# HGRN2 mixer of a decoder trunk: two heads in step, scores in 32-token blocks on four column groups, values and gates 512 columns wide

## The chip, the cores and the metric

The kernel runs on one core of one Trainium2 chip. Its time is the device time of one execution in microseconds (us); the median of three runs is given. A profile is of one execution. The engines are TensorE (PE in the profile; its weight loads are PEld), VectorE (DVE), ScalarE (ACT), GpSimd (POOL) and SyncE (SP), which here issues the DMAs. Each engine takes its instructions in the order in which they are written for it and waits on semaphores for the others.

## What is computed

Two layers over 512 tokens of 1024 features: a Mamba-2 mixer with an MLP and a gated embedding, then an HGRN2 mixer with the same two behind it. The change lies in the HGRN2 mixer, which has eight heads of 128 keys and 128 values:

```python
def hgrn2_mixer(u, w_in, lb, norm_w, w_out):
    q, fz, v, g = jnp.split(u @ w_in, 4, axis=-1)
    log_f = jnp.logaddexp(jnp.log(lb), jnp.log1p(-lb) + jax.nn.log_sigmoid(fz))
    k = (1.0 - lb) * jax.nn.sigmoid(-fz)
    ...
    def step(s_prev, inp):
        q_, kk, v_, b_ = inp
        diff = b_[:, :, None] - b_[:, None, :]
        dec = jnp.exp(jnp.where(mask, diff, -jnp.inf))
        scores = jnp.einsum('blhk,bshk,blshk->bhls', q_, kk, dec)
        o = jnp.einsum('bhls,bshv->blhv', scores, v_) + jnp.einsum('blhk,bhkv->blhv', q_ * jnp.exp(b_), s_prev)
        b_last = b_[:, -1]
        s_new = jnp.exp(b_last)[..., None] * s_prev + jnp.einsum(
            'bshk,bshv->bhkv', kk * jnp.exp(b_last[:, None] - b_), v_)
        return s_new, o
    ...
    o = rms_norm(o, norm_w).reshape(bsz, seq, D_MODEL) * jax.nn.silu(g.astype(jnp.float32))
    return o.astype(u.dtype) @ w_out
```

The score of a query token and an earlier key token is a sum over 128 keys of query times key times the product of all gates between the two. All arithmetic is fp32.

## The kernel before

Large products are made of three fp32r products each (`mm3`, lines 118 to 120): high part times high part, high times low, low times high. `unit` (L101) loads a weight tile of 128x1024 (512 KB) and splits it, ACT writing the high part `whi` (L112) and DVE the low part `wlo` (L114). There are three buffers for raw tiles and six each for `whi` and `wlo`. Tiles in the profile are named by their tags: `pj`, `py`, `pt`, `pm` are PSUM banks (four, two, one, one), `b` is a buffer of a split activation.

The mixer keeps 128 keys on the partitions and the 512 tokens along the free axis, in four chunks of 128. `qf` (L783) projects a head's queries and gates into tiles `xs` (q), `sz` (the gate f) and `cv` (k). `vg` (L762) projects values and gates for a pair of heads, with the activations as stationary operand and 256 weight columns moving (L775), and evacuates them by 512 columns (L777).

`hcore` (L846) works one head. It builds the scores of a chunk by levels: at level m, blocks of 2 to the m tokens are paired, and only the scores of a second block's queries with a first block's keys are new. In between the keys and queries of all blocks are multiplied by the gates' products (L912 for keys, L913 for queries, L916 for the products), so that a plain matrix product gives the decayed score.

- The diagonal and levels 0 and 1 are elementwise products, summed over the keys by a product with a matrix of ones, after a split (`column_sums`, L859; split at L861 and L862, product at L866).
- Levels 2 to 4 take full 128x128 products of a chunk in fp32 (`scores`, L852, product at L856), of which masks pick what is new (L927).
- Levels 5 and 6 (blocks of 32 and 64) multiply only the blocks needed (L901); ACT copies them (L931).
- Then keys are turned (L936, copied to `btok` at L938), states made (L943, L945, L947), outputs made (L954, L956), normalised and gated (L961 to L966), turned back (L972) and split (L973, L974).

What sets the order on TensorE is written out by hand: inside `manual_schedule` each `yield` of `hcore` tells how many us of background work to put there (`FILL`), and `fill` (L838) takes that much from `background` (L817): the projections of later heads, in the order of `JOBS`, and last `out0` (L803), the output projection of the first four heads. Two heads are worked at a time, an even one and an odd one at different stages. The order on the other engines is the scheduler's, with weight tiles pulled ahead. Behind the mixer come the output projection of the last four heads (L1003), the layer norm and the second MLP.

Of the kernel before, what the change touches and what calls it, by code (L numbers as in the profile page):

```python
# [9 lines left out]
F32R = mybir.dt.float32r  # L10
# [15 lines left out]
NLEV = 7  # L26
# [17 lines left out]
def trunk(ctx: ExitStack, tc, a):  # L44
# [30 lines left out]
    bufs = dict(ssd=dict(two, ss=2), mlp0=mlp, hgrn=dict(two, xs=4, sz=4, cv=4, y=2, pv=2, btok=2), mlp1=mlp)  # L75
# [667 lines left out]
    lmask = mk(cpool, [P, 6, P], "lmask", U8)  # L743
    lmf = mk(w4, [P, 6, P], "a")
    nc.sync.dma_start(lmf, a["lmask"])
    nc.vector.tensor_copy(lmask, lmf)
    ones_r = mk(cpool, [P, P], "ones_r", F32R)
    nc.scalar.activation(ones_r, ident, AF.Identity, scale=0.0, bias=one)
# [13 lines left out]
    def vg(i):  # L762

        res = []
        for which in range(2):
            units = [unit(a["whvg"][4 * i + 2 * which + j]) for j in range(2)]
            t = mk(w4, [P, NCH, 256], "ab"[which])
            for c2 in range(2):
                ps = bank(psj, "pj")
                for c in range(2):  # L770
                    sl = slice((2 * c2 + c) * P, (2 * c2 + c + 1) * P)
                    for k in range(8):
                        hi, lo = units[k // 4]
                        ks = slice((k % 4) * 256, (k % 4 + 1) * 256)
                        mm3(ps[:, c * 256 : (c + 1) * 256], x_s.h(k, sl), x_s.l(k, sl), hi[:, ks], lo[:, ks], k == 0, k == 7)  # L775
                        yield 0.33
                nc.scalar.activation(  # L777
                    t[:, 2 * c2 : 2 * c2 + 2, :].rearrange("p c f -> p (c f)"), ps, AF.Silu if which else AF.Copy
                )
            res.append(t)  # L780
        made["vg", i] = res

    def qf(h):  # L783
        ps = []
        for w in range(2):
            hi, lo = unit(a["whq"][2 * h + w])
            ps.append(bank(psj, "pj"))
            for k in range(8):
                c = slice(k * P, (k + 1) * P)
                mm3(ps[w], hi[:, c], lo[:, c], x_s.h(k), x_s.l(k), k == 0, k == 7)  # L790
                yield 0.65
            if w == 0:
                q = tmp("xs", [P, T])
                nc.scalar.copy(q, ps[0])
        f = tmp("sz", [P, T])
        nc.scalar.activation(f, ps[1], AF.Sigmoid)
        nc.scalar.activation(f, f, AF.Identity, scale=lbc[:, h : h + 1], bias=lb[:, h : h + 1])
        kk = tmp("cv", [P, T])
        nc.scalar.activation(kk, ps[1], AF.Sigmoid, scale=-1.0)
        nc.scalar.activation(kk, kk, AF.Copy, scale=lbc[:, h : h + 1])  # L800
        made["qf", h] = q, f, kk

    def out0():  # L803
        for h in range(2):
            units = [unit(a["who"][2 * h + i]) for i in range(2)]
            for c in range(NCH):
                sl = slice(c * P, (c + 1) * P)
                ps = bank(psj, "pj")
                for k in range(4):
# [3 lines left out]
                    yield 0.65  # L813
# [3 lines left out]
    def background():  # L817
        first = vg(0)
        for _ in range(FIRST_V):
            yield next(first)  # L820
        for f in late:
            f()
        yield from qf(0)
        yield from qf(1)
        yield from first
        for job in JOBS:
            yield from {"v": vg, "q": qf}[job[0]](int(job[1])) if job != "o" else out0()
# [18 lines left out]
    def hcore(h, s, i, hl):  # L846
        vs = slice((h % 2) * P, (h % 2 + 1) * P)
        q, f, kk = need("qf", h)
        sc = tmp("cm", [P, NCH, P])
        py = lambda: bank(psy, "py%d" % (h % 2))  # L850

        def scores():  # L852
            pc = py()
            for c in range(NCH):
                sl = slice(c * P, (c + 1) * P)
                nc.tensor.matmul(pc[:, sl], kk[:, sl], q[:, sl], start=True, stop=True)  # L856
            return pc.rearrange("p (c l) -> p c l", c=NCH)

        def column_sums(f, n):  # L859

            nc.scalar.copy(hl[:, 0, :n], f)  # L861
            nc.vector.tensor_sub(hl[:, 1, :n], f, f32(hl[:, 0, :n]))  # L862
            pc = py()
            yield FILL[0]
            for r in range(2):
                nc.tensor.matmul(pc[:, :n], ones_r, hl[:, r, :n], start=r == 0, stop=r == 1)  # L866
            return pc[:, :n].rearrange("p (c l) -> p c l", c=NCH)


        qk = tmp("cbm", [P, T])  # L870
        nc.vector.tensor_mul(qk, q, kk)
        nc.vector.tensor_mul(q, q, f)
        pc = yield from column_sums(qk, T)
        nc.vector.tensor_mul(sc, pc, bc(ident, 1, NCH))
        qk = tmp("cbm", [P, T])
        two = lambda t: t.rearrange("p (b two) -> p b two", two=2)
        nc.vector.tensor_mul(qk[:, : T // 2], two(q)[:, :, 1], two(kk)[:, :, 0])
        tot = f
        tots = tmp("y", [P, T])
        toff = 0  # L880
        for m in range(NLEV):
            half = 1 << m
            if m == 0:
                pc = yield from column_sums(qk[:, : T // 2], T // 2)
            elif m == 1:
                qk = tmp("cbm", [P, T])
                quads = lambda t: t.rearrange("p (b two u) -> p b two u", two=2, u=2)
                nc.vector.tensor_mul(
                    qk.rearrange("p (b l s) -> p b l s", l=2, s=2),
# [234 lines left out]
```

## Time and profile before

| | us |
|---|---|
| median of three runs | 1473.4 (1472.41 to 1473.43) |
| span of the profiled execution | 1471.1 |
| TensorE busy | 1455.5 |
| VectorE busy | 1076.6 |
| ScalarE busy | 731.8 |

The mean granted TensorE clock of the profiled execution is 0.998. The matmuls are pipelined: one of 128x512 is shown with about 0.39 us, while the next starts 0.227 us after it, so the work of TensorE is read from the starts. An fp32 matmul is shown as two records with a weight load each, an fp32r one as a single record.

### The profile page before, as it was taken

Reading aid. Unit: us, or ns where it says so; the run is one execution under the profiler, and the core shown is the slowest. Engines: PE = TensorE matmul, PEld = TensorE weight load, DVE = VectorE, ACT = ScalarE, POOL = GpSimd, SP = SyncE. Lnnn points to the kernel's source line nnn. Section 1 sums busy time; section 2 is a strip of 40 time slices with the busy share of each in tenths; the row PEclk is TensorE's granted clock in tenths of the full one; section 3 lists DMA queues with packets and bytes.
Section 4 is the critical chain, followed back from the end, with each engine's and each line's share of the span. In section 5 each row is a group of like instructions: output and inputs, shape, how many; then the busy total and the mean of one; then the engine's idle time right before and its main releaser. Section 6 shows DMA issues by size and latency. Waiting matters only on the chain.

```text
span 1471.1 us, 19578 instructions
## 1 busy us (share of the span) xinstructions
PE 1455.5 (99%) x7720; PEld 1223.5 (83%) x7720; DVE 1076.6 (73%) x1685; ACT 731.8 (50%) x1053; POOL 0.9 (0%) x9
## 2 busy tenths in 40 slices
PE   8999999999999999999999999999999999999998
PEld 6788888887888888888888998988888888888887
DVE  6999687787967667677845767768786766667873
ACT  5887455563264444545534453543346454444551
POOL 0000000000000000000000000000000000000000
PEclk9999999999999999999999999999999999999999
DMA  6343323233434434442413212222423434434231
GB/s 252 122 139 115 118 98 115 101 109 121 144 115 143 144 129 151 135 166 80 152 58 117 98 60 72 72 72 73 172 86 112 141 135 147 152 130 159 98 116 44
DMA packets 48381, 175.10 MB, mean 119 GB/s; under 512 B 5376, under 2 KB 5888, under 8 KB 48160
## 3 DMA queue, kind: packets, MB, share of 16 engines
q1 hardware_dynamic: 48288, 173.84, 34.9%
q8 instruction: 61, 1.00, 0.3%
q14 instruction: 32, 0.26, 0.1%
HBM read 171.66 MB, written 2.16 MB: 118 GB/s over the span
## 4 chain that ended last, share of the span: by engine, by line
PE 95%; DVE 3%; DMA 1%; ACT 1%; issue 0%; SPq 0%; ACTq 0%
PE pj L120 24%; PE pj L119 24%; PE pj L118 24%; PE py L119 4%; PE py L120 4%; PE py L118 4%; PE py L856 2%; PE py L664 1%; PE pm L634 1%; PE pt L227 1%; PE py L669 1%; DMA raw<-in_wssd 1%; PE py L866 1%; PE py L901 1%; PE pt L622 1%; DVE wlo L114 0%
## 5 line engine op out<-in xcount | busy, mean ns | idle before, releaser
L112 ACT CAST whi<-raw 128x1024 fp32r<-128x1024 f32 x224 | 234.6, 1050 | 372.1 <-PE pj L119 263.8
L118 PE MATMUL pj<-b,whi 128*128 128x512 f32 (+1 forms) x1008 | 383.9, 382 | 1.3 <-ACT b L231 1.3
L119 PE MATMUL pj<-b,whi 128*128 128x512 f32 (+1 forms) x1008 | 382.2, 380 | 0.0
L120 PE MATMUL pj<-b,wlo 128*128 128x512 f32 (+1 forms) x1008 | 381.9, 380 | 0.2 <-DVE wlo L114 0.2
L114 DVE TENSOR_TENSOR wlo<-raw,whi 128x1024 fp32r<-128x1024 f32 x224 | 272.3, 1220 | 137.5 <-ACT whi L112 135.0
L120 PE MATMUL pj<-whi,b 128*128 128x512 f32 (+1 forms) x720 | 252.5, 351 | 0.0
L118 PE MATMUL pj<-whi,b 128*128 128x512 f32 (+1 forms) x712 | 251.6, 353 | 0.5 <-ACT sg L481 0.5
L119 PE MATMUL pj<-wlo,b 128*128 128x512 f32 (+1 forms) x712 | 249.7, 351 | 0.0
L120 PEld LDWEIGHTS pj<-b,wlo 128*128 128x128 f32 x1008 | 190.7, 189 | 34.8 <-DVE wlo L114 0.6
L118 PEld LDWEIGHTS pj<-b,whi 128*128 128x128 f32 x1008 | 190.4, 189 | 34.7 <-ACT b L231 1.8
L119 PEld LDWEIGHTS pj<-b,whi 128*128 128x128 f32 x1008 | 190.8, 189 | 33.6 <-issue 1.0
L120 PEld LDWEIGHTS pj<-whi,b 128*128 128x128 f32 x720 | 136.2, 189 | 17.5 <-DVE b L974 0.2
L118 PEld LDWEIGHTS pj<-whi,b 128*128 128x128 f32 x712 | 134.7, 189 | 17.9 <-ACT sg L481 0.7
L119 PEld LDWEIGHTS pj<-wlo,b 128*128 128x128 f32 x712 | 134.8, 189 | 16.8
L112 ACT CAST whi<-r 128x1024 fp32r<-128x1024 f32 x64 | 67.4, 1054 | 63.7 <-PE pj L120 35.6
L114 DVE TENSOR_TENSOR wlo<-r,whi 128x1024 fp32r<-128x1024 f32 x64 | 78.1, 1220 | 18.9 <-ACT whi L112 18.7
L120 PE MATMUL py<-whi,b 128*128 128x512 f32 x216 | 84.1, 390 | 0.0
L119 PE MATMUL py<-wlo,b 128*128 128x512 f32 x192 | 74.7, 389 | 0.0
L118 PE MATMUL py<-whi,b 128*128 128x512 f32 x192 | 74.4, 389 | 0.0
L563 DVE SCALAR_TENSOR_TENSOR cv<-pj,cst,cv 128x509 f32<-128x509 f32 (+2 forms) x66 | 49.0, 743 | 5.0 <-ACT cv L560 4.5
L120 PEld LDWEIGHTS py<-whi,b 128*128 128x128 f32 x216 | 40.5, 188 | 8.5
L118 PEld LDWEIGHTS py<-whi,b 128*128 128x128 f32 x192 | 36.0, 188 | 7.7
(253 smaller groups left out, 1904.8 us busy)
## 6 DMA issues: line engine op xcount, KB each, us to landing
raw<-in_w SPq DMA_DIRECT2D x112, 512.0 KB, 3.5
r<-in_w SPq DMA_DIRECT2D x64, 512.0 KB, 4.0
raw<-in_wssd SPq DMA_DIRECT2D x36, 512.0 KB, 3.5
a<-csd SPq DMA_DIRECT2D x16, 512.0 KB, 3.8
raw<-in_wso SPq DMA_DIRECT2D x16, 512.0 KB, 3.4
raw<-in_wg SPq DMA_DIRECT2D x16, 512.0 KB, 3.5
raw<-in_whvg SPq DMA_DIRECT2D x16, 512.0 KB, 3.5
raw<-in_whq SPq DMA_DIRECT2D x16, 512.0 KB, 3.5
```

Of the source, the lines that this page charges most:

```text
L112: nc.scalar.copy(hi[:, :n], f)
L114: nc.vector.tensor_sub(lo[:, :n], f, f32(hi[:, :n]))
L118: nc.tensor.matmul(out, sh, mh, start=start, stop=False, **kw)
L119: nc.tensor.matmul(out, sh, ml, start=False, stop=False, **kw)
L120: nc.tensor.matmul(out, sl, mh, start=False, stop=stop, **kw)
L227: nc.tensor.transpose(pt[:, j * P : (j + 1) * P], src[:, k * P : (k + 1) * P], ident)
L563: nc.vector.scalar_tensor_tensor(cv[:, d:], ps[:, : T - d], convw[:, i, k : k + 1], cv[:, d:], ALU.mult, ALU.add)
L622: nc.tensor.transpose(pt[:, c * P : (c + 1) * P], xs[:, c * P : (c + 1) * P], ident)
L634: nc.tensor.matmul(pst_[:, c * P : (c + 1) * P], btok[:, c, :], xw[:, c].rearrange("p h q -> p (h q)"), start=True, stop=True)
L664: nc.tensor.matmul(yd[64 * r : 64 * r + 64, sl], xdt[:, 2 * c + r, :], m[:, r, sl], start=True, stop=True)
L669: nc.tensor.matmul(yo[:, c * P : (c + 1) * P], pv[:, c - 1].rearrange("p h q -> p (h q)"), cm[:, c * P : (c + 1) * P], start=True, stop=True,)
L856: nc.tensor.matmul(pc[:, sl], kk[:, sl], q[:, sl], start=True, stop=True)
```

## The change

The mixer's score part is written anew, in `heads(n, s)`, which takes both heads of pair n through the same steps one after the other.

- Queries are evacuated into a tile `qx` of 16 blocks with 80 columns each. The first 32 columns of a block are its queries; DVE writes 24, 16 and 8 more, queries that have been multiplied by the gates of one, two or three tokens before them (L872 to L874).
- Raw keys of a 32-token block times these 80 columns (L881) give all scores of tokens up to three apart in one product of 32x80, in the 32 PSUM partitions of that block. Four blocks make up a chunk and stand on four column groups of TensorE. The column sums, the ones matrix and the `T`-wide elementwise products are gone.
- Then keys and queries are brought to level 2 at once (L895 to L903), and the scores are picked into a tile `scd` of 32 columns a block (L908, L911).
- Levels 2 to 4 (blocks of 4, 8 and 16) multiply within 32-token blocks, 16 query columns at a time, again on four column groups (L933), and are picked by masked copies of 64 columns (L947). The updates stay as they were (L918, L919, L922).
- Levels 5 and 6 (L958) take the four chunks inside and the blocks in turn. ACT copies into `full`, whose rest was cleared once (L969, L972).
- Values and gates: `gated` projects 512 columns for two pairs at once (the products of `mm3` at 128x512), a bank for each chunk, and evacuates by 256 columns (L780). The first values go chunk by chunk, all others weight tile by weight tile. The job list names values and gates apart.
- Every `fill` amount is new. Background work is counted at 0.68 us a step rather than 0.65 (and 0.33 for 256 columns).

```diff
-JOBS = "q2 q3 v1 q4 q5 v2 q6 q7 v3 o".split()
-FILL = (2.0, 1.0, 1.3, 1.6, 2.3, 2.8)
-AHEAD = 6.0
-LAST = 0.78
-FIRST_V = 16
+JOBS = "g0 q2 q3 v1 q4 q5 g1 q6 q7 o".split()
+FILL = dict(gates=3.0, first=6.5, level=4.0, turn=3.5, state=2.5, out=3.5, norm=6.0, end=2.0)
+AHEAD = 3.0
...
+    def gated(i, which, by_chunk=False):
...
+        def part(c, j, un):
+            if j == 0:
+                ps[c] = bank(psj, "pj")
+            sl = slice(c * P, (c + 1) * P)
+            for k in range(2):
+                hi, lo = (v[:, k * 512 : (k + 1) * 512] for v in un)
+                mm3(ps[c], x_s.h(2 * j + k, sl), x_s.l(2 * j + k, sl), hi, lo, j == k == 0, j == 3 and k == 1)
+                yield 0.68
+            if j == 3:
+                for t, half in zip(pair, (0, 256)):
+                    nc.scalar.activation(t[:, c, :], ps[c][:, half : half + 256], AF.Silu if which else AF.Copy)
...
+    def heads(n, s):
...
+        for r in R:
+            vec.tensor_mul(rg(q[r][:, :, 32:56], 3), rg(q[r][:, :, 8:32], 3), fg[r][:, :, 1:4, :])
+            vec.tensor_mul(rg(q[r][:, :, 56:72], 2), rg(q[r][:, :, 40:56], 2), fg[r][:, :, 1:3, :])
+            vec.tensor_mul(q[r][:, :, 72:80], q[r][:, :, 64:72], fg[r][:, :, 1, :])
+        yield FILL["gates"]
+
+        pc = own()
+        for r in R:
             for c in range(NCH):
...
+                for b in range(4):
+                    nc.tensor.matmul(
+                        pc[r][32 * b : 32 * b + 32, 80 * c : 80 * c + 80],
+                        kk[r][:, 128 * c + 32 * b : 128 * c + 32 * b + 32],
+                        q[r][:, 4 * c + b, :],
+                        start=True,
+                        stop=True,
+                    )
...
+        for m in range(2, 5):
             half = 1 << m
...
+            for r in R:
+                for c in range(NCH):
+                    for b in range(4):
+                        ts = slice(128 * c + 32 * b, 128 * c + 32 * b + 32)
                         nc.tensor.matmul(
-                            pc[b : b + half, c, b + half : b + 2 * half],
-                            kk[:, s0 : s0 + half],
-                            q[:, l0 : l0 + half],
+                            pc[r][32 * b : 32 * b + 32, base + 16 * c : base + 16 * c + 16].rearrange(
+                                "p (n u) -> p n u", u=half
+                            ),
+                            kk[r][:, ts],
+                            second(qt[r][:, ts]),
                             start=True,
                             stop=True,
                         )
...
+            for r in R:
+                step(r, half)
+            for r in R:
+                to = small[r].rearrange("p c (n two u) -> p c n two u", two=2, u=half)[:, :, :, 1, :]
+                mv = masks[:, 48 + 16 * (m - 2) : 64 + 16 * (m - 2)].rearrange("p (n u) -> p n u", u=half)
+                vec.copy_predicated(
+                    to, bc(mv, 1, NCH), pc[r][:, base : base + 64].rearrange("p (c n u) -> p c n u", c=NCH, u=half)
+                )
+            yield FILL["level"]
...
+        for n in range(4):
+            if n % 2 == 0:
+                halves.append(Split(4))
+            for amount in heads(n, halves[-1]):
+                fill(amount)
         for _ in bg:
             pass
```

TensorE, at a level of the first pair of heads. Before, the full products of both heads (here level 3 of the even head and level 2 of the odd one) between products of the background, `pj`:

```order
L118 MATMUL pj_6840<-b_1004_5899,whi_6836 128x512
L119 MATMUL pj_6840<-b_1006_5901,whi_6836 128x512
L120 MATMUL pj_6840<-b_1004_5899,wlo_6838 128x512
L856 MATMUL py_1152_6869<-xs_6464,cv_6500 128x128 x4
L856 MATMUL py_1153_6878<-xs_6534,cv_6570 128x128 x4
L118 MATMUL pj_6840<-b_1005_5900,whi_6836 128x512
```

And now, where `mm3` stands at lines 115 to 117:

```order
L116 MATMUL pj_6662<-wlo_6789,b_1005_5900 128x512
L117 MATMUL pj_6662<-whi_6787,b_1007_5902 128x512
L933 MATMUL py_1140_6705<-qt_6739,k_6574 32x16 x16
L933 MATMUL py_1141_6706<-qt_6740,k_6644 32x16 x16
L115 MATMUL pj_6669<-whi_6787,b_1005_5900 128x512
L116 MATMUL pj_6669<-wlo_6789,b_1005_5900 128x512
```

Four products of 128x128 a head and level have become sixteen of 32x16, and the background's products are those of a gate projection with 512 weight columns moving.

TensorE, at the last pair: before, the background (`pj_8881` and `pj_8924` are parts of `out0`) still stood between the states (L943) and all that followed:

```order
L943 MATMUL pm_8909<-a_8320,btok_8875 128x128 x3
L118 MATMUL pj_8881<-whi_8849,b_1122_6650 128x512
L119 MATMUL pj_8881<-wlo_8851,b_1122_6650 128x512
L120 MATMUL pj_8881<-whi_8849,b_1123_6651 128x512
L118 MATMUL pj_8881<-whi_8849,b_1122_6650 128x512
L119 MATMUL pj_8881<-wlo_8851,b_1122_6650 128x512
L120 MATMUL pj_8881<-whi_8849,b_1123_6651 128x512
L118 MATMUL pj_8924<-whi_8843,b_1122_6650 128x512
```

Now (`pj_8998` belongs to the projection behind the mixer, its first half over heads 4 and 5):

```order
L116 MATMUL pj_8998<-wlo_8925,b_1273_7877 128x512
L117 MATMUL pj_8998<-whi_8923,b_1274_7878 128x512
L115 MATMUL pj_8998<-whi_8923,b_1273_7877 128x512
L116 MATMUL pj_8998<-wlo_8925,b_1273_7877 128x512
L979 MATMUL pt_8828<-cst_158,k_8293 128x128 x3
L117 MATMUL pj_8998<-whi_8923,b_1274_7878 128x512
L979 MATMUL pm_8829<-cst_158,k_8433 128x128 x3
L988 MATMUL py_1373_8840<-b_1195_7236,btok_8830 128x128 x3
L988 MATMUL py_1374_8841<-b_1195_7236,btok_8831 128x128 x3
L1004 MATMUL pt_8856<-b_1195_7236,sc_6350 128x128 x2
```

The background ends at level 4 of this pair. Products of the next projection stand between the last steps, and none between the turned keys (L979), the states (L988) and the outputs (L1004).

ScalarE, at the first pair's turned keys. Before, the copy to `btok` (L938) stood behind score copies and one weight cast:

```order
L931 COPY cm_6653<-py_1164_6968 64x4x64
L931 COPY cm_6687<-py_1165_6977 32x4x32 x2
L112 CAST whi_7410<-raw_7408 128x1024
L938 COPY btok_7004<-pt_7000 128x384
L931 COPY cm_6687<-py_1168_7006 64x4x64
```

Now a weight cast, a table load and the four gate activations of head 2 stand ahead of it:

```order
L109 CAST whi_7457<-raw_7455 128x1024
L810 ACT_TABLE_LOAD
L810 ACTIVATE f_7089<-pj_7048 128x512
L813 ACTIVATE k_7092<-pj_7048 128x512
L811 ACTIVATE f_7089<-f_7089,lb_6360,lbc_6362 128x512
L814 ACTIVATE k_7092<-k_7092,lbc_6362 128x512
L980 COPY btok_7107<-pt_7105 128x384
L980 COPY btok_7108<-pm_7106 128x384
```

The copy moved behind the activations that wait for the last product of `pj_7048`, the gate projection of head 2.

More of the change, by code (lines that the diff above doesn't have):

```diff
@@ L25 @@
 EPS = 1e-5
-NLEV = 7
 LEAD = 100
@@ L977, in trunk @@
+        yield FILL["norm"]
+        pt = own()
+        for r in R:
+            i = (2 * n + r) % 4
+            for c in range(NCH):
+                nc.tensor.transpose(pt[r][:, c * P : (c + 1) * P], o[r][:, c, :], ident)
+            nc.scalar.activation(s.h(i), pt[r], AF.Copy, scale=hnw[:, 0:1])
+            vec.scalar_tensor_tensor(s.l(i), pt[r], hnw[:, 0:1], f32(s.h(i)), ALU.mult, ALU.subtract)
+        yield FILL["end"]
     halves = []
     with tc.manual_schedule(engines={mybir.EngineType.PE}):
-        need("qf", 1)
+        need("q", 1)
```

352 lines of the change are left out of this document (166 added, 186 removed).

## The prediction

> **What bounds the kernel now.** I read the page first (busy shares, chain of work that ended last), then the windows of the stage that the change touches, then TensorE's timeline there, and last the groups by shape. Columns of a group's row: line, engine, operation, out<-in, shapes, count | busy us, mean ns | idle before it.
>
> ```profile
> PE 1455.5 (99%) x7720; PEld 1223.5 (83%) x7720; DVE 1076.6 (73%) x1685; ACT 731.8 (50%) x1053; POOL 0.9 (0%) x9
> PE 95%; DVE 3%; DMA 1%; ACT 1%; issue 0%; SPq 0%; ACTq 0%
> ...
> 980.00:1000.00 20.00, 19.75 (x162) 19.12 (x161) 13.58 (x37) 12.71 (x33) 0.00 (x0) 1.00 0.19 60
> 1000.00:1020.00 20.00, 19.45 (x138) 17.93 (x137) 17.13 (x32) 6.43 (x9) 0.00 (x0) 1.00 0.35 126
> 1060.00:1080.00 20.00, 20.00 (x126) 17.83 (x124) 19.98 (x30) 7.52 (x11) 0.00 (x0) 1.00 0.29 107
> ...
> 1084.00:1088.00 4.00, 2.12 (x17) 1.70 (x15) 4.00 (x5) 0.35 (x1) 0.00 (x0) 1.00 0.38 132
> 1088.00:1092.00 4.00, 2.98 (x17) 2.77 (x18) 3.97 (x4) 0.82 (x2) 0.00 (x0) 0.79 0.00 0
> ```
>
> The windows' columns are: stretch, its length, busy us of PE, PEld, DVE, ACT, POOL, then granted clock and DMA. TensorE (PE) works without a pause through the HGRN mixer (777 to 1049 us); only 0.25 and 0.55 us are missing at 980 to 1020. The first real pause comes after it, in the layer norm (1.9 and 1.0 us at 1084 to 1092, some 1.4 us more lost to the granted clock of 0.79), where DVE is full. So what counts is TensorE's time in the mixer and any wait put in its place. As TensorE never rests, an instruction's price is the distance from its start to the next start, not its duration.
>
> **What goes.** Timeline rows: start, us, engine, line, operation.
>
> ```profile
> 815.51 0.28 PE L118 MATMUL pj<-whi,b 128*128 128x256 f32 x1
> 815.63 0.28 PE L119 MATMUL pj<-wlo,b 128*128 128x256 f32 x1
> ...
> 819.81 0.85 PE L866 MATMUL py<-b,ones_r 128*128 128x256 f32 x4
> 820.50 0.28 PE L118 MATMUL pj<-whi,b 128*128 128x256 f32 x1
> ...
> 833.95 0.39 PE L119 MATMUL pj<-b,whi 128*128 128x512 f32 x1
> 834.18 0.39 PE L120 MATMUL pj<-b,wlo 128*128 128x512 f32 x1
> 834.41 2.14 PE L856 MATMUL py<-xs,cv 128*128 128x128 f32 x16
> 836.31 0.48 PE L118 MATMUL pj<-b,whi 128*128 128x512 f32 x1
> ...
> L118 PE MATMUL pj<-whi,b 128*128 128x256 f32 x272 | 77.8, 286 | 0.5 <-ACT sg L481 0.5
> L856 PE MATMUL py<-xs,cv 128*128 128x128 f32 x192 | 25.0, 278 | 0.6 <-DVE cm L925 0.6
> ```
>
> - Values and gates: 256 of the 272 products of each kind are theirs (16 belong to the last gate, L478), 768 in all, 0.12 us apart: 92.2 us. At 512 columns they are 384, at the 0.227 us of 833.95 to 834.18: 87.2 us. **-5.0 us.**
> - Column sums (L866): the four at 819.81 are two of 256 and two of 512 columns and take 0.69 us; a head has two more of 512 (0.45 us). 8 x 1.15 = **-9.2 us.**
> - Full 128x128 scores of levels 2 to 4 (L856): 16 in 1.90 us, 0.119 each; 192 of them: **-22.8 us.** (An fp32 product is two records.)
>
> Together 37.0 us.
>
> **What comes.** Narrow products exist in the trace: 32 columns in one column group after another (L901), 64 in one group (L901 again) and in two taken in turn (L694), and four groups in turn (L502, with 512 columns).
>
> ```profile
> 842.07 0.39 PE L120 MATMUL pj<-b,wlo 128*128 128x512 f32 x1
> 842.39 0.59 PE L901 MATMUL py<-xs,cv 128*32 128x32 f32 x16
> 842.91 1.16 PE L856 MATMUL py<-xs,cv 128*128 128x128 f32 x8
> ...
> 849.85 0.68 PE L901 MATMUL py<-xs,cv 128*64 128x64 f32 x8
> 850.46 0.50 PE L118 MATMUL pj<-b,whi 128*128 128x512 f32 x1
> 850.80 0.40 PE L119 MATMUL pj<-b,whi 128*128 128x512 f32 x1
> ...
> 139.28 0.69 PE L694 MATMUL pm<-ones_s,ss 128*64 128x64 f32 x16
> 139.89 0.50 PE L119 MATMUL pj<-wlo,b 128*128 128x512 f32 x1
> ...
> 20.55 0.59 PE L502 MATMUL pj<-a,raw 128*32 128x512 f32 x1
> ...
> 20.57 0.59 PE L502 MATMUL pj<-b,raw 128*32 128x512 f32 x1
> 20.98 0.59 PE L502 MATMUL pj<-a,raw 128*32 128x512 f32 x1
> ```
>
> Eight records in one group take 0.61 us (849.85 to 850.46), sixteen in two groups taken in turn take the same 0.61 us (139.28 to 139.89); with four groups, four records start within 0.02 us and the next four 0.43 us later. Groups taken in turn run side by side, and the new code takes them in turn.
>
> - Raw scores (L881 after): 8 heads x 16 products x 2 records = 256 in 64 sets of four. A set of 512 columns costs 0.43 us, so one of 80 costs 0.067: **+4.3 us** (serial: 17.2).
> - Levels 2 to 4 (L933 after): 8 x 3 x 32 = 768 records of 16 columns. At the pace of 842.39 to 842.91 (16 in 0.52 us, 0.032 each) they cost 24.6 us; with four side by side a quarter, 6.2. No run of the trace issues records closer than that 0.032 us over more than one such burst, so how fast 64 in a row can follow is open. I take the middle in ratio, 0.016 each: **+12.3 us** (6.2 to 24.6).
> - Going in and out of narrow shapes: 842.07 to 842.39 is 0.09 over the 0.227 us, and 850.46 to 850.80 is 0.11 over on the way out; with the first record's slow start I take 0.25 us a visit. There are 16 new visits (one raw, three levels, for each of four pairs), and the visits of the two widest levels fall from 16 to 8 as both heads share one: +4.0 - 2.0 = **+2.0 us.**
>
> Together 18.6 us, so TensorE's work falls by **18.4 us.** The rest (transposes, states, outputs) keeps its count.
>
> **What the other engines do beside it.** They hide their edits as long as the fill between two steps (3 to 6.5 us) covers them.
>
> ```profile
> L912 DVE TENSOR_TENSOR cv<-cv,y 128x256 f32<-128x256 f32 x48 | 20.2, 422 | 11.9 <-PE py L856 6.6 <-PE py L901 4.7
> ...
> L938 ACT COPY btok<-pt 128x384 f32<-128x384 f32 x8 | 3.9, 481 | 0.3
> ...
> 840.91 1.05 ACT L112 CAST whi<-raw 128x1024 fp32r<-128x1024 f32 x1 [9.10 <-PE pj L119]
> 841.98 1.28 ACT L796 ACT_TABLE_LOAD   x1
> ...
> 845.56 0.51 ACT L931 COPY cm<-py 32x128 f32<-32x128 f32 x2
> ...
> 1037.24 0.60 PE L954 MATMUL py<-a,cm 128*128 128x128 f32 x4
> ...
> 1038.80 0.83 PE L943 MATMUL pm<-a,btok 128*128 128x128 f32 x6
> ...
> 1045.32 0.28 ACT L961 ACTIVATE cbm<-py 128x128 f32<-128x128 f32 x1 [0.88 <-PE py L956]
> ...
> 1046.50 0.30 ACT L962 ACTIVATE hms<-hms,cst 128x4 f32<-128x4 f32 x1
> ...
> 1047.04 1.13 DVE L966 SCALAR_TENSOR_TENSOR cbm<-py,hri,b 128x128 f32<-128x128 f32 x4
> ...
> 1049.72 0.68 ACT L973 ACTIVATE b<-pt,cst 128x512 fp32r<-128x512 f32 x1
> ...
> 1051.36 0.74 DVE L974 SCALAR_TENSOR_TENSOR b<-pt,cst,b 128x512 fp32r<-128x512 f32 x1
> ```
>
> DVE loses the products and splits ahead of the column sums and the 512-wide masked copies, and gains narrow ones; a level's four updates (0.42 us each, L912) and two masked copies of 64 columns are about 2.3 us against 4.0 us of fill. ACT loses the casts ahead of the column sums and gains small copies and 256-wide evacuations. Both cost nothing while covered. The same bytes are loaded; the first values need four weight tiles rather than two by the end of their first chunk, which I put at nothing, as their buffers come free while the stage before still multiplies (uncovered: a wait for one tile's landing and split).
>
> Three places are not covered:
> - The copy of the turned keys (ACT) now stands behind a weight cast, a table load and the four gate activations of the pair to come. The same six run today from 840.91 to 845.56, 4.65 us; with the copy's 0.48 they take 5.1. The fill against it is 18 products and the six transposes, 18 x 0.227 + 0.7 = 4.8. TensorE's state products, and all behind them, wait about 0.3 us, without the table load not at all. With small misses elsewhere: **+1.5 us** over four pairs.
> - The last pair. The background runs out at its level 4, and 24 products of the next projection are all that fills the rest. From there to the last split I add: three rounds of updates and scores 6.0 (each two heads' updates, 1.7, and the products they wait for); transposes, two copies and states 2.6; both heads' outputs 2 x 1.56 (1037.24 to 1038.80) = 3.1; then, the first head's squares lying under the second's outputs, table 1.28, root 0.3, the second's squares 1.2 (1045.32 to 1046.50) and root 0.3, less 0.4 of overlap, 2.7; scaling to 1.7 after the root (1046.50 to 1048.17); turning back 0.5, scaled copy 0.68, split 0.74: together 18 us. TensorE has 8.3 of the pair's own (28 output, 12 state and 14 transpose records at 0.112, and 2.2 for the two wide levels), 5.4 of fill and 1.5 at the end to do in it: **+2.8 us** idle (0 to 8).
> - Behind it, the layer norm's pauses of 4.3 us (1084 to 1092, the clock's loss included). It will have 24 products less to lie under DVE's chain, but that chain starts earlier, since the first two chunks need only half their products by then; I take 3.3 us (0 to 8). With the 0.8 us of waits at 980 to 1020 gone too: **-1.8 us.**
>
> Net waits +2.5 us. The profiled execution spans 1471.1 us and the median of the three runs is 2.3 above it; I move both alike. Span 1471.1 - 18.4 + 2.5 = 1455.2, and median 1473.4 - 15.9 = **1457.5 us.**
>
> **A rule against it.** The Trainium skill ("TensorE: Matmul & The Clock Gate", part 1, "Wait — 56ns, not 53.3ns?") says that start-to-start never drops below about 25 ns however few columns a product has. An estimate by that page: 768 x 25 = 19.2 and 256 x 25 = 6.4 us instead of 12.3 and 4.3, hence 1466.5. The four starts within 20 ns in the L502 rows speak against it between groups; a long run of such starts is not in this trace.
>
> **The rivals.**
> - *Issue-bound*: 64 short records in a row come no faster than the closest long burst seen, 0.032 us each (842.39). Levels 24.6, raw scores 8.2: 16.2 us more, 1474; with a pace between, 1466 to 1474. For it: nothing denser is shown. Against: L502's starts.
> - *Waits take the saving's place*: ACT's copy and DVE's updates come late at every pair (2 us each) and the last chain is bare (8 us): about 11 us more, 1469. For it: in-order ACT with 4.65 us ahead of the copy. Against: DVE has 2.9 to 6.4 us free in each 20 of the mixer's windows.
> - *Slower*: the four groups do not overlap for products this short, as each must load weights of its own before it runs. Raw scores 17.2, levels 24.6: 25.2 us more, 1483. It decides if fewer than 1.3 of the four run at a time, for then 41.8/1.3 = 32 us eats the 15.9. For it: the 16 of 842.39 gain little from two groups. Against: L694 against L901, exactly twofold.
>
> **How the numbers follow.** Forecast 0.64 (its own range 1450 to 1466: levels at 6.2 and no waits, or 5 us more waits and 3 us more levels); issue-bound 0.16; waits 0.10; serial 0.10. The range takes in all but the last: 1449 to 1474. A measurement can tell 0.2% (3 us) from no change: faster means below 1470.5, where the forecast, two thirds of the second and most of the third case lie, 0.82; within it 0.08; slower 0.10.
>
> **What would show it.** Right: L881's records in fours a few ns apart and sets 0.07 us on; a level's visit (64 records) of about 1.0 us; 0.12 us products gone from the mixer; mixer's windows of PE full until the last pair. Wrong: a level's visit of 2 us (serial or issue-bound, told apart by whether the four starts bunch), idle TensorE ended by ACT's btok or DVE's k at each pair, a pause above 5 us before the layer norm, or a granted clock under 1.00 inside the mixer.

## The result and the profile after

| | before | after |
|---|---|---|
| median of four executions, us | 1473.3 (1472.41 to 1473.43) | 1445.63 (1445.45 to 1446.54) |
| span of the profiled execution, us | 1471.1 | 1443.9 |
| mean granted TensorE clock | 0.998 | 1.000 |

The medians lie 27.7 us apart. The ratio is 0.9818, with a 95% interval of 0.9806 to 0.983, which makes 26.8 us less than before. The forecast was 1457.5 us, 15.9 less, and the time lies below the low end of the range (1449). The direction and the main mechanism were right, and the gain was about 1.7 times what was forecast.

First the changed kernel's page, busy times of the engines and the chain that ended last, then its windows (stretch, length, busy us of PE, PEld, DVE, ACT, POOL, granted clock, DMA). The layer norm behind the mixer lies at 1040 to 1067 us now.

```profile
PE 1430.9 (99%) x8120; PEld 1181.0 (82%) x8120; DVE 1039.3 (72%) x1661; ACT 732.5 (51%) x1076; POOL 1.9 (0%) x11
...
PE 95%; DVE 2%; ACT 1%; DMA 1%; issue 0%; SPq 0%; ACTq 0%
```

```profile
980.00:1000.00 20.00, 20.00 (x165) 16.93 (x165) 14.62 (x38) 11.47 (x29) 0.00 (x0) 1.00 0.16 54
1000.00:1020.00 20.00, 20.00 (x303) 15.61 (x301) 17.02 (x46) 6.54 (x13) 0.00 (x0) 1.00 0.26 81
1020.00:1030.00 10.00, 9.39 (x70) 7.87 (x67) 4.09 (x12) 6.74 (x27) 0.00 (x0) 1.00 0.35 131
1030.00:1040.00 10.00, 9.74 (x42) 7.35 (x43) 8.37 (x20) 2.27 (x7) 0.00 (x0) 1.00 0.89 343
1040.00:1060.00 20.00, 20.00 (x135) 18.05 (x134) 19.72 (x31) 8.30 (x13) 0.00 (x0) 1.00 0.12 39
1060.00:1080.00 20.00, 19.96 (x150) 18.99 (x149) 19.84 (x20) 11.13 (x15) 0.00 (x0) 1.00 0.46 148
```

TensorE is still the bound. In the mixer it rests for two waits of 0.24 us before its last pair; the tail of that pair (1020 to 1040) is the one place with more idle time, and in the layer norm, where 2.9 us and a clock of 0.79 stood before, 0.04 us is missing, at full clock. The waits of TensorE between 780 and 1100 us (who waits <- for whom: us in all, times, longest) are, by that view, only these:

```profile
PE py L1025 <- DVE o L1016: 0.9, 2, 0.6
PE py L988 <- ACT btok L980: 0.5, 2, 0.2
```

From the starts the tail loses some 2.5 us: the last pair's first six transposes at L1025 take 2.65 us, 2.0 more than in the pairs before, and its states and outputs 0.5 more.

The second wait is for the copy of the turned keys, and ScalarE's timeline shows it where the prediction put it: weight cast, table load, four activations, then the copy.

```profile
859.72 1.05 ACT L109 CAST whi<-raw 128x1024 fp32r<-128x1024 f32 x1 [3.03 <-PE pj L116]
860.79 1.28 ACT L810 ACT_TABLE_LOAD   x1
...
864.38 0.47 ACT L980 COPY btok<-pt 128x384 f32<-128x384 f32 x1
```

It occurs in the first and third pair alone, those with a table load. There the 12 state products and their way in and out take 0.5 us longer than in the second pair (TensorE's starts).

The new products, on TensorE's timeline (start, us, engine, line, operation):

```profile
827.32 0.39 PE L117 MATMUL pj<-whi,b 128*128 128x512 f32 x1
827.64 1.31 PE L881 MATMUL py<-qx,k 128*32 128x80 f32 x64
828.88 0.50 PE L115 MATMUL pj<-whi,b 128*128 128x512 f32 x1
...
835.59 0.39 PE L117 MATMUL pj<-whi,b 128*128 128x512 f32 x1
835.91 0.74 PE L933 MATMUL py<-qt,k 128*32 128x16 f32 x64
836.57 0.50 PE L115 MATMUL pj<-whi,b 128*128 128x512 f32 x1
836.91 0.40 PE L116 MATMUL pj<-wlo,b 128*128 128x512 f32 x1
```

A visit is the time from the background product ahead to the next start behind, less that product's own 0.227 us, and what the product behind is slower: for a level (835.59 to 836.57 to 836.91) 0.98 - 0.227 + 0.11 = 0.866 us; for the raw scores 1.445. From the first of its 64 records to the start of the product behind them it is 0.66 and 1.24 us.

### The profile page after: what moved, and what is told of

Read it like the earlier page. It is cut to its first block, busy times and chain, and to the rows that moved or that the text cites. A ratio compares the mean times of both kernels' runs of the same rounds, so it can differ in the third digit from the quotient of the medians.

```text
span 1443.9 us, 20344 instructions
## 1 busy us (share of the span) xinstructions
PE 1430.9 (99%) x8120; PEld 1181.0 (82%) x8120; DVE 1039.3 (72%) x1661; ACT 732.5 (51%) x1076; POOL 1.9 (0%) x11
## 4 chain that ended last, share of the span: by engine, by line
PE 95%; DVE 2%; ACT 1%; DMA 1%; issue 0%; SPq 0%; ACTq 0%
PE pj L115 25%; PE pj L116 24%; PE pj L117 24%; PE py L116 5%; PE py L117 5%; PE py L115 5%; PE py L661 1%; PE pm L631 1%; PE pt L224 1%; PE py L666 1%; DMA raw<-in_wssd 1%; PE py L933 1%; PE pt L619 1%; PE py L958 0%; PE py L988 0%; DVE wlo L111 0%
## 5 line engine op out<-in xcount | busy, mean ns | idle before, releaser
L117 PE MATMUL pj<-whi,b 128*128 128x512 f32 (+1 forms) x592 | 230.5, 389 | 0.0
L115 PE MATMUL pj<-whi,b 128*128 128x512 f32 (+1 forms) x584 | 229.8, 394 | 0.5 <-ACT sg L478 0.5
L116 PE MATMUL pj<-wlo,b 128*128 128x512 f32 (+1 forms) x584 | 227.4, 389 | 0.0
L117 PEld LDWEIGHTS pj<-whi,b 128*128 128x128 f32 x592 | 111.2, 188 | 22.4 <-issue 0.2
L115 PEld LDWEIGHTS pj<-whi,b 128*128 128x128 f32 x584 | 109.7, 188 | 23.3 <-ACT sg L478 0.7
L116 PEld LDWEIGHTS pj<-wlo,b 128*128 128x128 f32 x584 | 109.8, 188 | 21.1
L109 ACT CAST whi<-r 128x1024 fp32r<-128x1024 f32 x64 | 67.4, 1053 | 63.8 <-PE pj L117 35.6
L111 DVE TENSOR_TENSOR wlo<-r,whi 128x1024 fp32r<-128x1024 f32 x64 | 78.1, 1220 | 21.5 <-ACT whi L109 21.3
```

Source lines behind the costliest of these rows:

```text
L109: nc.scalar.copy(hi[:, :n], f)
L111: nc.vector.tensor_sub(lo[:, :n], f, f32(hi[:, :n]))
L115: nc.tensor.matmul(out, sh, mh, start=start, stop=False, **kw)
L116: nc.tensor.matmul(out, sh, ml, start=False, stop=False, **kw)
L117: nc.tensor.matmul(out, sl, mh, start=False, stop=stop, **kw)
```

## The experiments

Times are medians. The changed kernel gave 1445.63 and, run again (`e11_after_again`), 1446.37 us; where nothing else is said, differences are taken from their middle, 1446.0. A ratio's interval is about 0.0013 to either side, some 1.9 us. What is below that is told from the traces.

**Column groups, one after another, and two in turn.**

```diff
-            for c in range(NCH):
-                for b in range(4):
+            for b in range(4):
+                for c in range(NCH):
```

(at L879 and L930; in the second kernel the order is groups 0 and 1 in turn for all chunks, then 2 and 3)

> The changed kernel with the narrow products of L881 and L933 issued one column group after another instead of the four in turn. The same products, the same order of everything else. Theory A (groups in turn run side by side; a product of 32 weight columns holds its own group for 32 ns however few columns it multiplies): a level's visit becomes 64 x 0.032 + 0.2 = 2.25 us instead of 0.866, and a raw visit, by 0.119 us for 128 columns, 64 x 0.074 + 0.2 = 4.9 instead of 1.445; 12 x 1.4 + 4 x 3.5 = +31 us, about 1476 us. Theory B (short products are cheap by their size alone, about 10 ns each, and the groups play no part): visits stay at 0.87 and 1.45 us, 1445 to 1447 us.

> The changed kernel with the narrow products of L881 and L933 issued to two column groups in turn, first groups 0 and 1, then 2 and 3. Theory A: half as fast as with four groups in the limit of 32 ns for a group: a level's visit 64 x 0.016 + 0.2 = 1.23 us, a raw visit 64 x 0.037 + 0.2 = 2.6 us; 12 x 0.36 + 4 x 1.15 = +9 us, about 1454.5 us. This is the pace of 0.016 us that the prediction took for the levels. Theory B: no change, 1445 to 1447 us. If four groups already stood at a limit of issue near 10 ns a record rather than of the groups, two groups would show the group's own time, twice it or less.

Measured: 1461.71 us one after another (ratio to before 0.9928, 0.9913 to 0.9942), +15.7; 1450.71 us with two in turn (0.985, 0.9836 to 0.9865), +4.7. TensorE's timelines, of the first and then of the second kernel:

```profile
828.30 2.89 PE L881 MATMUL py<-qx,k 128*32 128x80 f32 x64
831.12 0.50 PE L115 MATMUL pj<-whi,b 128*128 128x512 f32 x1
...
838.14 1.50 PE L933 MATMUL py<-qt,k 128*32 128x16 f32 x64
839.57 0.50 PE L115 MATMUL pj<-whi,b 128*128 128x512 f32 x1
```

```profile
828.08 1.69 PE L881 MATMUL py<-qx,k 128*32 128x80 f32 x64
829.70 0.50 PE L115 MATMUL pj<-whi,b 128*128 128x512 f32 x1
...
836.72 0.92 PE L933 MATMUL py<-qt,k 128*32 128x16 f32 x64
837.57 0.50 PE L115 MATMUL pj<-whi,b 128*128 128x512 f32 x1
```

The same 64 records take 0.66, 0.85 and 1.43 us (16 columns) and 1.24, 1.62 and 2.82 us (80 columns) with four groups, two and one. So the groups do it, and theory B falls. But both runs cost only half of what theory A expected. The starts of single records show why (ns from one start to the next, the first twelve steps of a burst):

```
16 columns, four in turn    6  7  7 32  7  6  7 12  6  7  7 11
16 columns, group by group 53 32 31 32  6 26 26  5 27  5 27 31
80 columns, four in turn    6  7  7 73  7  6  7 49  7  7  6 49
80 columns, group by group 93 69 69 70  5 64 30 39 30 39 30 69
```

Within one group records follow every 32 ns (16 columns) or 69 ns (80 columns), and a record of another group 5 to 7 ns after the last. Where the group changes, the records of both are interleaved (26, 5, 27, 5): a group's first record is shown with 203 ns and the others with 183, and the second group's first stands 6 ns behind the fifth of the first group's eight. So some overlap is there even one group after another: 22 ns a record instead of 32. Theory A is right in kind; its sum left that overlap out.

**The price of 64 more records, and of one more visit.**

```diff
-        for r in R:
+        for r in (0, 0, 1, 1):
```

(at L878 and L929, all products twice to the same place)

> The changed kernel with each head's 32 products of L881 and of L933 issued twice in a row to the same place, the outputs unchanged: what 64 more records cost without going in and out again. Theory A (about 10 ns a record of 16 columns, 19 ns one of 80): a level's visit 0.866 + 0.66 = 1.53 us, a raw visit 1.445 + 1.24 = 2.69 us; 12 x 0.66 + 4 x 1.24 = +12.9 us, about 1458.5 us. Rival (the prediction's pace, 0.016 and 0.017 us a record, the first burst being cheap because its weights were loaded under the products ahead of it): 12 x 1.02 + 4 x 1.08 = +16.6 us, 1462 us. Rival (a visit is mostly a fixed cost): under +5 us.

```diff
+                if r == 0:
+                    yield 0.68
...
-            yield FILL["level"]
+            yield FILL["level"] - 0.68
```

(behind L941 and at L950)

> The changed kernel with one background product (three records of 512 columns) between the first and the second head's 16 products of L933, taken from the fill behind the level: 12 more visits of narrow shapes, the same work. Theory A (going in and out costs 0.2 us a visit, read as 0.866 less the 0.66 us of the records): 12 x 0.2 = +2.4 us, 1448.0 us. The prediction's 0.25 us: +3.0 us, 1448.6 us. Rival (the visit's 0.866 us are the records' own and going in and out is free): 0, 1445.6 us.

Measured: twice 1457.23 us (+11.2), in two visits 1449.53 us (+3.5). First the timeline with the products twice, then the first of a level's two visits:

```profile
827.22 2.42 PE L881 MATMUL py<-qx,k 128*32 128x80 f32 x128
829.57 0.50 PE L115 MATMUL pj<-whi,b 128*128 128x512 f32 x1
...
842.14 1.29 PE L933 MATMUL py<-qt,k 128*32 128x16 f32 x128
843.36 0.50 PE L115 MATMUL pj<-whi,b 128*128 128x512 f32 x1
```

```profile
840.82 0.45 PE L933 MATMUL py<-qt,k 128*32 128x16 f32 x32
841.20 0.50 PE L115 MATMUL pj<-whi,b 128*128 128x512 f32 x1
```

Sixty-four more records cost 1.22 - 0.66 = 0.56 us at 16 columns (8.7 ns each) and 2.35 - 1.24 = 1.11 at 80 (17 ns each, 69 for a set of four). The rest of a visit, 0.866 - 0.56 and 1.445 - 1.11, is some 0.3 us for going in and out; two visits of 32 records take 2 x 0.58 us against 0.866, once more 0.29. So theory A's split (0.66 of records, 0.2 of going in and out) had the right sum with 0.1 us on the wrong side, and the prediction's 0.25 us a visit was a little low. Its pace of 16 ns falls.

**Values and gates 256 columns wide.**

```diff
-                mm3(ps[c], ..., hi, lo, ...)
+                for w in (slice(0, 256), slice(256, 512)):
+                    mm3(ps[c][:, w], ..., hi[:, w], lo[:, w], ...)
```

> The changed kernel with each product of values and gates taken as two of 256 columns in the same place, 768 instead of 384. By the prediction's term (0.120 us for 256 columns, 0.227 for 512): 768 x 0.120 - 384 x 0.227 = +5.0 us, 1450.6 us. Rival (the pace of a 256-column product rises to its half, 0.1135, when nothing stands between): 0 us.

Measured: 1451.33 us, +5.3. The term of 5.0 us holds.

**The price of what was removed, by doubling it in the kernel before** (L856 and L866 there, each product issued twice).

> The kernel before with the full 128x128 scores (L856, 192 records) and the column sums (L866, 48 products of fp32r) each issued twice to the same place, the results unchanged: the price of what the change removes, by doubling it. By the prediction's terms: 22.8 + 9.2 = +32.0 us, 1504.5 us. Rival (part of the mixer's products lay in time that TensorE would have spent waiting): less, by what is hidden.

Measured: 1501.18 us, ratio 1.0195 (1.0181 to 1.0209), +28.6 us. The rows of the first full scores that were doubled there (with L857 and L867 for L856 and L866):

```profile
832.60 1.95 PE L857 MATMUL py<-xs,cv 128*128 128x128 f32 x16
834.30 1.18 PE L867 MATMUL py<-b,ones_r 128*128 128x512 f32 x4
```

Sixteen records and the step to the product behind them take 1.70 us there. From start to start the records are 0.112 us apart, and by the starts a visit of 16 alone takes 1.79 us (in the kernel before), one of 32 takes 3.58: nothing is added for going in and out of 128x128 products. The 0.119 that the prediction read holds 0.2 us of longer steps in the middle of the one visit at 834.41, which five of the eight visits of that size do not have. 192 x 0.112 = 21.5, with 9.2 for the sums 30.7; all doubled visits together take 30.0 us more by the starts, and the time rose by 28.6. So the two terms stand within some 2 us, the interval's width, and little of the doubled work lay in idle time.

**The layer norm.** By TensorE's starts, the eight visits to the norm's transposes took 7.4 us before and take 3.8 now, of which 0.25 is one wait (ahead of L224 at 1064.02); and before, the wide products behind the last of them took 1.4 us longer, at a lowered clock. That is 4.9 us less now. The prediction counted 4.3 us before (2.9 of waits and those 1.4), without the slowed visits themselves, and expected 3.3 to stay. VectorE's timeline at the end of the norm, of the kernel before and then of the changed one:

```profile
1084.43 1.22 DVE L319 TENSOR_TENSOR r<-r,r 128x1024 f32<-128x1024 f32 x1
1085.57 1.28 DVE L218 SCALAR_TENSOR_TENSOR acc<-acc,lnrs,b 128x1024 f32<-128x1024 f32 x1
1086.76 1.22 DVE L321 TENSOR_TENSOR r<-r,r 128x1024 f32<-128x1024 f32 x1
1087.90 1.22 DVE L325 TENSOR_TENSOR r<-r,r 128x1024 f32<-128x1024 f32 x1
1089.03 0.68 DVE L232 TENSOR_TENSOR b<-pt,b 128x512 fp32r<-128x512 f32 x1
1089.63 1.21 DVE L322 TENSOR_TENSOR r<-r,r 128x1024 f32<-128x1024 f32 x1
1090.88 1.23 DVE L325 TENSOR_TENSOR r<-r,r 128x1024 f32<-128x1024 f32 x1
1092.02 0.68 DVE L232 TENSOR_TENSOR b<-pt,b 128x512 fp32r<-128x512 f32 x1
```

```profile
1063.28 0.68 DVE L229 TENSOR_TENSOR b<-pt,b 128x512 fp32r<-128x512 f32 x1
1063.88 2.35 DVE L316 TENSOR_TENSOR r<-r,r 128x1024 f32<-128x1024 f32 x2
1066.15 0.68 DVE L229 TENSOR_TENSOR b<-pt,b 128x512 fp32r<-128x512 f32 x1
1066.75 2.35 DVE L318 TENSOR_TENSOR r<-r,r 128x1024 f32<-128x1024 f32 x2
```

The `r` rows are sums of weights for the second MLP, 1.13 us each, which nobody needs yet. Before, all eight stood ahead of the norm's last split (L232 at 1092.02), three of them early in the norm and five in its last part (the texts below count seven, without the one that ends as the split starts); in the changed kernel two do. The change does not touch them; the scheduler placed them anew. Two runs tell whether that is the cause.

```diff
+                if behind is not None:
+                    e = t[0][u][:, 0:1]
+                    nc.vector.scalar_tensor_tensor(e, f32(behind), 0.0, e, ALU.mult, ALU.add)
```

(in the kernel before, in `weight_sums` ahead of its first sum, for the second MLP's first block; `behind` is a column of what the norm's last split writes)

> The kernel before, with the second MLP's first sums of weights (eight operations of VectorE, 1.13 us each, seven of which end before the layer norm's last split there, at 1092 us) made to wait for that last split by a product with zero of one column; values unchanged, nothing of the change in it. Theory A (the pause of the layer norm is VectorE's, and went in the changed kernel because these sums moved behind the splits): the pause of 4.3 us at 1084 to 1092 falls to under 1 us and the time by 3 to 4 us, 1469.5 us. Theory B (it went because the layer norm starts earlier against TensorE's work, its first chunks needing only half their products): the pause stays within 1 us of 4.3, 1472.5 to 1473.5 us.

Measured: 1467.67 us, ratio 0.9968 (0.9955 to 0.998), -4.65 us. The windows of this kernel, without a pause and at full clock:

```profile
1084.00:1088.00 4.00, 4.00 (x35) 3.90 (x34) 1.91 (x5) 1.17 (x2) 0.00 (x0) 1.00 0.08 31
1088.00:1092.00 4.00, 4.00 (x35) 4.00 (x35) 4.00 (x4) 1.68 (x3) 0.00 (x0) 1.00 0.00 0
```

The kernel before could have had 4.65 us by that alone. Theory A holds there. The reverse, in the changed kernel:

```diff
+                for _ in range({(2, 1): 3, (2, 3): 4}.get((i, c), 0)):
+                    nc.vector.tensor_tensor(acc[:, c, :], acc[:, c, :], acc[:, c, :], ALU.max)
                 layer_norm(c, gb, sums)
```

> The changed kernel with the second MLP's first sums of weights held behind the layer norm's last split (as in e6_before_sums_late) and seven operations of VectorE of their size (the maximum of a chunk with itself, 128x1024, no value changed) put into the layer norm's chain, three at its second chunk and four at its fourth, where the kernel before had seven sums and the changed kernel two: the reverse of e6_before_sums_late. Theory A (the pause is VectorE's order alone): the pause of 2.9 us idle and a lowered clock of the kernel before is back, +3.5 to +5.5 us, about 1450 us. Theory B (the change's order of products gives the layer norm more room, and the sums did not matter in it): under +1 us, 1446 to 1447 us. Between: what each is worth.

Measured: 1460.05 us, ratio 0.9911 (0.9897 to 0.9925), +14.1 us, far over both theories. Its waits and two windows:

```profile
PE pt L224 <- DVE acc L215: 4.2, 1, 4.2
PE pt L224 <- DVE lnrs L212: 3.4, 1, 3.4
```

```profile
1050.00:1060.00 10.00, 6.74 (x32) 6.37 (x33) 9.04 (x12) 1.47 (x3) 0.00 (x0) 0.66 0.16 52
1070.00:1080.00 10.00, 5.42 (x24) 5.05 (x25) 5.91 (x11) 1.47 (x3) 0.00 (x0) 0.67 0.00 0
```

It is no clean reverse: the seven operations depend on the chunk and so lengthen the norm's chain itself, where the sums had partly lain in its gaps. It shows that seven operations more in the norm's chain (7 x 1.13 = 7.9 us) find no room in the changed kernel, so theory B's time did not come; how much of the vanished pause is due to the order of the sums there it does not tell. It also shows that a pause costs more than its length: TensorE's eight visits to the norm's transposes (L224) take 11.8 us more than in the changed kernel, and the wide products between them some 3 us more, at half clock (0.66 and 0.67 are means over windows of 10 us; narrower ones, 1053 to 1059.6 and 1073.5 to 1080, show 0.50).

**What is left.** Other fills, and then those with the sums of weights held back too:

```diff
+FILLS = [dict(FILL, level=3.86, turn=4.2), FILL, dict(FILL, level=3.86, turn=4.2),
+         dict(FILL, level=3.0, first=6.0)]
...
+        FILL = FILLS[n]
```

> The changed kernel with other amounts of background work: in the first and third pair of heads 4.2 us instead of 3.5 behind the turning of the keys, taken from the five levels (3.86 instead of 4.0 each); in the last pair 3.0 instead of 4.0 behind each level and 6.0 instead of 6.5 behind the raw scores, so that some 5 us of products move from its front to its tail. If the two waits for the turned keys' copy (0.5 us each, in the pairs with a table load) and the idle 2.5 us of the tail are what is left of the waits, and VectorE's updates stay under 3 us of fill: -1 and -2 us, 1442.5 us. Rival (the last pair's chain is VectorE's throughout, and the pause only moves forward): -1 us or less, 1444.5 to 1446 us.

> The changed kernel with the fills of e7_fills, except 3.4 (not 3.0) behind each level and 6.5 behind the raw scores in the last pair, and with the second MLP's first sums of weights made to wait for the layer norm's last split, as in e6_before_sums_late. In e7_fills two waits appeared where the others went: 0.7 us in the layer norm (L225 for VectorE's split) and 0.3 us at a level (L935 for VectorE's masked copy). If they are VectorE's order and the fill of 3.0 alone: both go, and the time falls by 1 us more, 1443.5 us, 2 us under the changed kernel. Rival (what leaves the tail comes back in the layer norm in any order): 1444.5 us, as e7_fills.

> The changed kernel itself, on the same chip as e8_fills_sums_late and e9_widest_group_by_group, for the small differences: 1445.5 to 1446.5 us.

Measured: 1444.46 us (0.9814, 0.98 to 0.9827) and 1444.72 us (0.9812, 0.9799 to 0.9825); the changed kernel beside the second, 1446.37. TensorE's waits, of the first and of the second:

```profile
PE pt L225 <- DVE b L230: 0.7, 1, 0.7
PE py L935 <- DVE scd L949: 0.3, 1, 0.3
```

```profile
PE py L1031 <- DVE o L1022: 0.3, 1, 0.3
PE pt L985 <- DVE k L924: 0.2, 1, 0.2
```

The waits for the turned keys are gone in both, and the times are 1.5 and 1.7 us lower, half and four fifths of what was expected and close to what the rivals gave. In the first, the last pair's tail is 1.9 us shorter by TensorE's starts, and part of that came back in the layer norm and at a level. In the second nothing came back in the layer norm, but the tail is only 0.2 us shorter (the first six transposes of the last pair, L1031 there, still take 2.1 us, against 2.65), so its fills had left most of the idle time in place. That run is therefore no test of what the sums are worth. These differences are within the interval, so a version that is measurably better than the changed kernel was not found.

**The level of 32, group by group.**

```diff
-                for c in range(NCH):
-                    for b in range(0, P, 2 * half):
+                for b in range(0, P, 2 * half):
+                    for c in range(NCH):
```

(at L955)

> The changed kernel with the products of the level of 32 (L958, 128 records of 32 columns) issued one column group after another, as the kernel before did, instead of two groups in turn: 32 records of a visit (both heads) take 0.63 us now. Theory A (one group holds 32 ns a record, with some overlap where the group changes, as 16 records in 0.52 us of the kernel before show): 32 x 0.031 = 1.0 us, +0.37 us a visit, +1.5 us over four pairs, 1447.1 us; part of the gain that the prediction had not counted in the other products of the mixer. Rival (that gain is only in fewer visits): 0.

Measured: 1446.91 us, +0.5 beside the changed kernel on the same chip, no difference that the runs can tell. In the trace a visit's 32 records take 0.83 us instead of 0.63, so turns of two groups are worth 0.2 us a visit, 0.8 us in all, half of what was expected, again because of the overlap where the group changes.

```profile
851.60 0.90 PE L958 MATMUL py<-qt,k 128*32 128x32 f32 x32
852.43 0.50 PE L115 MATMUL pj<-b,whi 128*128 128x512 f32 x1
```

## Why the prediction was too cautious, by its own steps

| step | forecast, us | measured, us |
|---|---|---|
| values and gates at 512 columns | -5.0 | -5.3 (e5) |
| column sums and full scores gone | -32.0 | -31.5 by TensorE's starts; 28.6 to double them (e10) |
| raw scores, 256 records | +4.3 | +4.4 (4 x 1.11) |
| levels 2 to 4, 768 records | +12.3 | +6.7 (12 x 0.56) |
| going in and out, 16 new visits | +4.0 | +5.0 (12 x 0.31, 4 x 0.33) |
| the mixer's other visits | -2.0 | -3.9 (what is left) |
| wait for the turned keys | +1.5 | +1.0 |
| idle in the last pair's tail | +2.8 | +2.5 |
| layer norm's pause | -1.0 | -4.9 |
| waits at 980 to 1020 gone | -0.8 | -0.8 |

With the first term at its forecast, the right column is 10.6 us under the left one: by it the span would be 1455.2 - 10.6 = 1444.6 us. The two profiled executions of the changed kernel span 1443.9 and 1444.6. The row of the other visits is what is left of TensorE's narrow visits (69.0 us in the mixer before, 52.4 now) once the other rows are taken out, so the agreement is no test of that row.

- **The step that failed most is the pace of the levels.** The prediction had the mechanism (four column groups side by side) and with it the number, a quarter of 0.032 us, 6.2 us in all; it then took "the middle in ratio, 0.016 each", since no row showed a long burst that dense. The runs show 8.7 ns, 5.6 us less. The raw scores, where a row of the same kind (L502) was carried through, came out at 69 ns a set against the 67 forecast. That row's factor of four should have been trusted for the levels too. Its scaling by columns would not have held there: 16 of 512 columns of 0.43 us are 13 ns a set, and the steps show 32, the time that one record holds its group.
- **The second is the layer norm.** "It will have 24 products less to lie under DVE's chain" was weighed against an earlier start of that chain. In the kernel before, the pause went without either (e6). What was on VectorE ahead of the last split was not looked at: eight sums that the scheduler could place either way. That they can be worth 4.65 us is shown in the kernel before; that they account for all of the 4.9 us in the changed one is the likeliest reading, and was not shown by itself.
- **The mixer's other visits** gained 1.9 us more than forecast. Those with products of 32 and 64 columns (L901, now L958) took 11.7 us before by the starts and take 8.4 now, the last pair's wait left out: 3.3 of the 3.9. The turns of two groups at the level of 32 are 0.8 of that (read in e9's trace). The prediction counted 16 such visits before; the trace has 12, as two heads at neighbouring levels share one. Where the rest comes from was not tried apart.
- **Right** were the removed work, the wide products, going in and out (0.25 against 0.3 us a visit), the place and cause of the wait for the turned keys, and the tail: from the last level's products (1015.65) to the last split's end (1034.27) 18.6 us against the 18 that were added up.

All larger misses but one pointed the same way; going in and out cost 1.0 us more than forecast. The range's low end, 1449, goes with the levels at their low bound and net waits of nothing (1457.5 - 6.1 - 2.5 = 1448.9): it gave the layer norm no gain beyond what the change's own waits would take.

Three rivals are settled by the traces. Waits did not take the saving's place: those of the turned keys and of the last pair's tail came to 3.5 us against the 16 of that rival, and VectorE's updates caused none at the levels. Issue at 0.032 us a record and serial groups are both out: the densest steps are 5 to 7 ns, and a single group gives 32. The Trainium skill ("TensorE: Matmul & The Clock Gate", part 1, "Wait — 56ns, not 53.3ns?") states a floor of about 25 ns from start to start; this trace disagrees for products that go to different column groups (8.7 ns on average, for 64 records) and does not contradict it for those of one group (32 ns).

## What to carry to other kernels

Where products need few weight columns, put them on different column groups and issue the groups in turn: a group is then the unit that is held, and four short products cost what one does, plus some 0.3 us for each time TensorE leaves its wide products for them. When a bound from a mechanism and a bound from what has been seen stand apart, test which row of the profile is of the same kind, rather than take the middle. Before a pause is forecast to stay, list what the engine that ends it has in its queue that could as well come later.

## What the runs showed of the hardware that was not expected

- Records of one column group follow after 32 ns with 16 columns and with 32, and after 69 ns with 80: below some width a product of 32 weight columns is not cheaper. Records of another group start 5 to 7 ns later, and a second 64 in the same burst still add only 8.7 ns each.
- Where a program changes from one group to the next, the records of both are interleaved, so that even an order without turns has two fifths to a half of the overlap: 22 ns a record for 16 columns, 44 for 80.
- In the layer norm the granted clock fell to 0.50: for 6.8 us each, from about the end of pauses of 3.4 and 4.2 us (e12), and for 3.4 us behind three waits of 1.5, 0.7 and 0.7 us (before, 1090.3 to 1093.7; the 0.79 of the 4 us window is a mean). With waits of 0.7 and 0.3 us, far apart, it stayed at 1.00 (the first run of other fills). Idle time so cost about 1.6 times its length: 14.1 us for 9.0 of waits in e12, 4.65 us for 2.9 in the kernel before, by e6.
